# Seven-product units for retention's q/k and gates, with the residual kept in DRAM and two raw weight buffers instead of three

## The chip, the cores and the metric

One NeuronCore of a Trainium2 chip runs the whole program. The metric is device time in microseconds (us). The kernel before takes 2482.47 us (median of 3 runs, 2482.29 to 2485.35).

## What is computed

Two transformer blocks, one behind the other, on 512 tokens of width 1024, all in float32:

```python
# first block, two layers
h = h + stick_breaking_attention(rms_norm(h, g), w_sb_in, w_sb_out)
h = h + squared_relu_mlp(rms_norm(h, g), w_up, w_down)      # 1024 -> 4096 -> 1024
h = h + retention(rms_norm(h, g), w_ret_in, w_ret_out)      # 4 heads: q, k 256 wide, v and gate 512 wide
h = h + squared_relu_mlp(rms_norm(h, g), w_up, w_down)
h = rms_norm(h, g_final)
# second block
x = x + 0.5 * swiglu_ffn(x, ...)                            # hidden width 2816
x = x + mixer(x)                                            # sparse attention and mLSTM, gated
x = x + 0.5 * swiglu_ffn(x, ...)
```

## The kernel before, in words

Activations are kept transposed: tiles of 128 features by 512 tokens, in one pool of `HEAP` tiles of 2 KB a partition (L25). Every float32 operand is split into a high and a low part, and a product is three matmuls (`mm3`, L124 to L127: hi by lo, lo by hi, hi by hi).

**Weights.** `build` (L1667) lists all weight panels in the order of their use. A panel is 1 MB as a rule and is loaded by SP into one of `RAWS` raw buffers of 8 KB a partition (`load_ahead`, L193, L201). `prep` (L216) makes the high part on ACT (L240) and the low part on DVE (L241), in two halves of 1024 columns.

**A direct unit** (`g_unit`, L284) multiplies one 1024 x 128 block of weights by all 512 tokens: 8 x 3 = 24 matmuls of 512 columns. Two of them use up a panel.

**A seven-product unit** (`w_unit`, L326) does the same two blocks at once by a Strassen-Winograd scheme on 2 x 2 blocks: 7 products of 4 x 3 matmuls with 256 columns, accumulated in four PSUM banks (`w_banks`, L293, all four `z` banks). It needs sums of weight quarters and sums of activation halves. The weight sums are made partly by DMA: four loads on SP (L206 to L209), then two accumulating DMAs on POOL (L210, L211), which wait for the loads and give S1 and S3; then two DVE sums (L263) for S2 and S4. ACT (L272) and DVE (L232) split each of the seven operands. `prep` may run `WAHEAD` = 5 products ahead. The activation sums (`T`, 16 heap tiles for 1024 features) are made at the head of a stage by `w_operands` (L302): lift, four DVE sums of 256 columns, two ACT and two DVE operations of 512 (L319, L320), four times.

**Where each is used.** In each MLP (L539) the first of four groups of eight up-units is direct, and `w_operands` is spread over it, one step every `WT` = 3 atoms (an atom is three matmuls, or six in a seven-product unit); groups 1 to 3 are seven-product. In each SwiGLU (`ffn`, L995) the first `GC` = 4 gate/up pairs are direct, the other 18 are seven-product. Retention (`ret`, L853) is all direct: for each head `proj` (q, k by `g_unit`, v by `g_tokens`) and `gate` (four `g_unit`), with a `chain` woven in at one step every 4 atoms: six steps of `scores`, then sixteen of `values`, of which the last two are the row sums (L444) and, after a reciprocal square root on DVE, their spread (L437). What is left of a chain when the next head's `proj` ends is run at once (`drain`). `out(0)` (heads 0 and 1) comes after `gate(2)`, `out(1)` at the end; both add to the residual tiles `hh` (L894).

The order written in the code is a priority: the framework's scheduler issues each engine's instructions as their inputs, and the heap or raw slots they write, come free; an engine then runs them in that fixed order. A slot is taken by the first write to a tile. At the start the input `x` is loaded into two tiles of the raw pool (L1718), between the pieces of the first panel.

Of the kernel before, what the change touches and what calls it, by code (L numbers as in the profile page):

```python
# [7 lines left out]
F32 = mybir.dt.float32  # L8
# [7 lines left out]
S = 512  # L16
D = 1024
KT = 8
# [3 lines left out]
DROP = -3.3e38  # L22
FAR = -1.0e30

HEAP = 70  # L25
HALVES = 4
RAWS = 3
DEPTH = 2
LAG = 4
N1 = 6  # L30
# [24 lines left out]

WAHEAD = 5

WT = 3

GC = 4  # L60


CHUNKS = {
# [23 lines left out]
class Builder:  # L87
    def __init__(self, tc, d, out, pools):
        self.tc, self.nc, self.d, self.out = tc, tc.nc, d, out
        self.cp, self.wp, self.hp, self.sp, self.pp = pools  # L90
# [12 lines left out]
        self.uid = 0  # L103
        self.stop_at = None
# [176 lines left out]
        self.pos += 1  # L281
        return p

    def g_unit(self, name, X, w=None):  # L284
        w = w or self.next(name)
        ps = self.ps("m")
        n = len(X)
        for k in range(n):
            self.mm3(ps, w[:, k * 128:(k + 1) * 128], X[k], k == 0, k == n - 1)
            yield  # L290
        self.last = ps
# [66 lines left out]
                    yield  # L358
        self.later(done[3], c, lag=1)

    def g_tokens(self, name, X, done):

        pss = [self.ps("z" if i == ZT else "m") for i in range(4)]
# [175 lines left out]
    def mlp(self, layer, hh, X, box, nxt):  # L539

        nc = self.nc
        st = {}
        self.norm_soon(st, box)
        U = {}


        def up_done(m, ps):
            z = self.h()
            nc.scalar.activation(z, ps, AF.Relu)
            nc.scalar.activation(z, z, AF.Square)  # L550
# [36 lines left out]
        banks = self.w_banks(X[0].hi)  # L587

        def main():
            for grp in range(4):  # L590
                for m in range(0, 8, 2):
                    if grp == 0:
                        for x in range(2):
                            yield from self.g_unit(f"up{layer}", X[::2] + X[1::2])
                            self.later(up_done, m + x, self.last)
                    else:
                        yield from self.w_unit(f"up{layer}", T, banks, pair_done(m))
                if grp == 0:
                    for _ in ops:
                        pass  # L600
                self.flush()
                W = [U[m] for m in range(8)]
                for m in range(8):
                    yield from self.g_unit(f"dn{layer}", W)
                    self.later(down_done, grp, m, self.last)

        self.weave(main(), [[ops, WT]])
        self.flush()

# [240 lines left out]
                                         fill=0.0, base=0, channel_multiplier=-1)  # L850


    def ret(self, hh, X, box, nxt):  # L853
        nc = self.nc
        st = {}
        self.norm_soon(st, box)
        cs, sn = self.h(), self.h()
# [6 lines left out]
        self.later(tables, lag=N2)  # L864
        Q, V, G, SC, Y = {}, {}, {}, {}, {}

        def rotate(h, which, p1, p2):
            f = 1.0 if which == 0 else 1.0 / 16
            ts = [self.h() for _ in range(4)]
            for t, p, c in zip(ts, (p1, p2, p1, p2), (cs, sn, sn, cs)):  # L870
                nc.vector.scalar_tensor_tensor(t, p, f, c, ALU.mult, ALU.mult)
            nc.vector.tensor_tensor(ts[0], ts[0], ts[1], ALU.subtract)
            nc.vector.tensor_tensor(ts[2], ts[2], ts[3], ALU.add)
            Q[h, which] = [self.split(ts[0]), self.split(ts[2])]

        def v_done(h):
            def done(tt, ps):
# [7 lines left out]
                self.later(ev)  # L885
            return done

        def g_done(h, c, ps):
            f = G[h, c] = self.h()
            nc.vector.tensor_tensor(f, ps, st["R"], ALU.mult)  # L890
            nc.scalar.activation(f, f, AF.Silu)
# [6 lines left out]
        def scores(h):  # L898
# [20 lines left out]
        def values(h):  # L919
            sq = []  # L920
            for et in range(4):
                ps = self.ps("z")
# [25 lines left out]
        def out(pair):  # L948
            W = [Y[2 * pair + x, et] for x in range(2) for et in range(4)]
            for m in range(8):  # L950
                yield from self.g_unit("reto", W)
                self.later(out_done, pair == 1, m, self.last)

        def proj(h):
            for which in range(2):
                yield from self.g_unit("retqk", X)
                p1 = self.last
                yield from self.g_unit("retqk", X)
                self.later(rotate, h, which, p1, self.last)
            yield from self.g_tokens("retv", X, v_done(h))  # L960

        def gate(h):
            for c in range(4):
                yield from self.g_unit("retg", X)
                self.later(g_done, h, c, self.last)

        def chain(h):
            yield from scores(h)
            while (h, 3) not in G:
                yield  # L970
            yield from values(h)

# [694 lines left out]
    def build(self):  # L1667
# [8 lines left out]

        def mlp(l):
            for g in range(4):
                P(f"up{l}", range(g * 4, g * 4 + 4), g > 0)
                P(f"dn{l}", range(g * 4, g * 4 + 4))  # L1680

        def ffn(w):
# [6 lines left out]

        mlp(0)  # L1690
        for h in range(4):
            P("retqk", [2 * h, 2 * h + 1])
            P("retv", [2 * h, 2 * h + 1])
            P("retg", [2 * h, 2 * h + 1])
            if h >= 2:
                P("reto", range((h - 2) * 4, (h - 2) * 4 + 4))
        mlp(1)
# [15 lines left out]
        P("wo", range(4))  # L1713
        ffn(2)

        self.setup()

        self.xraw = [self.wp.tile([128, 2048], F32, name="raw", tag="raw", bufs=RAWS) for _ in range(2)]  # L1718
# [37 lines left out]
        if stop == "mlp0":  # L1756
            return hh
        X, Y = [], X
        self.ret(hh, Y, box, ready("mlp1", X, hh))
        if stop == "ret":  # L1760
            return hh

# [22 lines left out]

        def residual():
            R1 = self.bcast(st["r1"])
            for kt in range(KT):
                nc.vector.scalar_tensor_tensor(hh[kt], hh[kt], self.g("fin", kt), R1, ALU.mult, ALU.mult)
        self.later(two_norms, lag=N1)  # L1790
        self.later(spread_r, lag=N2)
        X, Y = [], X
# [41 lines left out]
def layout(x, w_sb_in, w_sb_out, w_ret_in, w_ret_out, g_mix, g_mlp, w_mlp_up, w_mlp_down, g_final,  # L1834
# [33 lines left out]
    d["retqk"] = full(qk.reshape(1024, 2048))  # L1868
    d["retv"] = _tok(w[:, 2048:4096])
    d["retg"] = full(w[:, 4096:])  # L1870
# [55 lines left out]
def trace(tc, d, out, stop=None, manual=False):  # L1926
    import contextlib

    with contextlib.ExitStack() as st:
        pool = lambda name, **kw: st.enter_context(tc.tile_pool(name=name, **kw))  # L1930
        pools = (pool("const", bufs=1), pool("weights", bufs=2), pool("heap", bufs=HEAP), pool("small", bufs=24),
                 pool("psum", bufs=1, space=bass.MemoryType.PSUM))
        if manual:
            st.enter_context(tc.manual_schedule())
        b = Builder(tc, d, out, pools)
# [21 lines left out]
```

## Time and profile before

| | |
|---|---|
| median of 3 runs | 2482.47 us |
| the profiled execution: time, span | 2483.38 us, 2481.7 us |
| TensorE (PE) busy | 2458.5 us, 99% of the span, 13679 matmuls |
| VectorE (DVE) busy | 1723.5 us, 69% |
| ScalarE (ACT) busy | 1253.1 us, 50% |
| GpSimd (POOL) busy | 138.1 us, 6% |
| DMA | 273.20 MB, mean 110 GB/s |

Busy times of PE are modelled (matmuls overlap one another), so its speed is read from the starts of successive matmuls. The time of an execution is 1.7 us longer than the span, which is from the first to the last instruction.

### The profile page before, as it was taken

The page shows a single profiled execution, that of the slowest core. Times are in us where ns is not written, and L with a number is a line of the kernel's source. Part 1 is how long each engine was busy: PE and PEld are TensorE (multiplying, and loading weights), DVE is VectorE, ACT ScalarE, POOL GpSimd, SP SyncE. Part 2 cuts the span into 40 slices and gives each one's busy share as a digit, 9 for nine tenths or more (in the row PEclk, how much of TensorE's full clock was granted, in tenths as well). Part 3 has the DMA queues.
Part 4 walks back from the last instruction along what each step waited for, and adds up shares of the span by engine and source line. Part 5 has one row for each costly group of instructions (what it writes and reads, how often), then busy time and mean ns, then how long its engine had stood idle before and what let it go on. Part 6 is the DMA issues. An engine that isn't in the chain of part 4 may idle for free.

```text
span 2481.7 us, 35229 instructions
## 1 busy us (share of the span) xinstructions
PE 2458.5 (99%) x13679; PEld 2141.8 (86%) x13679; DVE 1723.5 (69%) x3061; ACT 1253.1 (50%) x2160; POOL 138.1 (6%) x242
## 2 busy tenths in 40 slices
PE   9999999999999999999999999999999999999999
PEld 7888789989888888889989899998877888899998
DVE  7878857657655545657657776768799777666765
ACT  6777655436333323445436544545555454544543
POOL 0000000000000000000000001010000000001010
PEclk9999999999999999999999999999999999999999
DMA  4112144444222222244443445553221122445551
GB/s 172 69 52 85 51 136 129 127 140 131 95 89 86 76 85 98 76 132 131 129 132 127 119 139 158 148 151 115 73 85 68 51 69 85 123 141 157 150 149 73
DMA packets 78511, 273.20 MB, mean 110 GB/s; under 512 B 8836, under 2 KB 9220, under 8 KB 60680
## 3 DMA queue, kind: packets, MB, share of 16 engines
q1 hardware_dynamic: 60912, 239.43, 27.4%
q0 software_dynamic: 17280, 31.46, 7.7%
q8 instruction: 107, 1.75, 0.3%
q14 instruction: 60, 0.49, 0.1%
q10 hardware_dynamic: 152, 0.06, 0.0%
HBM read 268.82 MB, written 2.10 MB: 109 GB/s over the span
## 4 chain that ended last, share of the span: by engine, by line
PE 93%; DVE 3%; ACT 2%; issue 1%; DMA 0%; SPq 0%; DVEq 0%; ACTq 0%
PE ps_m L125 20%; PE ps_m L126 20%; PE ps_m L127 20%; PE ps_z L125 9%; PE ps_z L127 9%; PE ps_z L126 9%; PE ps_z L134 1%; PE ps_z L796 1%; PE ps_o L437 1%; DVE wlo L241 1%; PE ps_z L135 1%; PE ps_z L797 1%; PE ps_o L444 1%; ACT whi L240 0%; DVE h L1399 0%
## 5 line engine op out<-in xcount | busy, mean ns | idle before, releaser
L125 PE MATMUL ps_m<-h,whi 128*128 128x512 f32 (+1 forms) x2114 | 831.2, 393 | 7.1 <-DVE h L1191 3.5
L126 PE MATMUL ps_m<-h,wlo 128*128 128x512 f32 (+1 forms) x2114 | 826.0, 391 | 0.0
L127 PE MATMUL ps_m<-h,whi 128*128 128x512 f32 (+1 forms) x2114 | 825.0, 390 | 0.0
L240 ACT ACTIVATE whi<-raw 128x1024 fp32r<-128x1024 f32 (+2 forms) x297 | 309.7, 1043 | 580.8 <-PE ps_m L127 493.4
L125 PEld LDWEIGHTS ps_m<-h,whi 128*128 128x128 f32 x2114 | 398.1, 188 | 89.3 <-issue 6.6
L241 DVE TENSOR_TENSOR wlo<-raw,whi 128x1024 fp32r<-128x1024 f32 (+2 forms) x297 | 357.0, 1202 | 166.2 <-ACT whi L240 131.8
L127 PEld LDWEIGHTS ps_m<-h,whi 128*128 128x128 f32 x2114 | 398.1, 188 | 83.3
L126 PEld LDWEIGHTS ps_m<-h,wlo 128*128 128x128 f32 x2114 | 398.5, 189 | 76.9 <-issue 1.2
L125 PE MATMUL ps_z<-h,whi 128*128 128x256 f32 x840 | 237.8, 283 | 1.2 <-ACT h L345 1.2
L125 PE MATMUL ps_z<-h,wlo 128*128 128x256 f32 x840 | 237.7, 283 | 0.0
L126 PE MATMUL ps_z<-h,wlo 128*128 128x256 f32 x840 | 237.7, 283 | 0.0
L127 PE MATMUL ps_z<-h,whi 128*128 128x256 f32 x840 | 237.7, 283 | 0.0
L127 PE MATMUL ps_z<-h,wlo 128*128 128x256 f32 x840 | 237.7, 283 | 0.0
L126 PE MATMUL ps_z<-h,whi 128*128 128x256 f32 x840 | 237.7, 283 | 0.0
L125 PEld LDWEIGHTS ps_z<-h,whi 128*128 128x128 f32 x840 | 161.2, 192 | 1.8 <-ACT h L345 1.4
L126 PEld LDWEIGHTS ps_z<-h,whi 128*128 128x128 f32 x840 | 161.2, 192 | 0.4
L125 PEld LDWEIGHTS ps_z<-h,wlo 128*128 128x128 f32 x840 | 161.3, 192 | 0.0
L126 PEld LDWEIGHTS ps_z<-h,wlo 128*128 128x128 f32 x840 | 161.3, 192 | 0.0
L127 PEld LDWEIGHTS ps_z<-h,wlo 128*128 128x128 f32 x840 | 161.3, 192 | 0.0
L127 PEld LDWEIGHTS ps_z<-h,whi 128*128 128x128 f32 x840 | 161.2, 192 | 0.0
L580 DVE TENSOR_TENSOR h<-ps_m,h 128x512 f32<-128x512 f32 x64 | 44.3, 692 | 152.7 <-PE ps_m L127 152.7
L272 ACT ACTIVATE wlo<-raw 128x512 fp32r<-128x512 f32 x120 | 75.0, 625 | 148.8 <-PE ps_m L126 127.9
(338 smaller groups left out, 3664.8 us busy)
## 6 DMA issues: line engine op xcount, KB each, us to landing
raw<-dn SPq DMA_DIRECT2D x32, 1024.0 KB, 4.8
raw<-gu SPq DMA_DIRECT2D x72, 256.0 KB, 4.4
raw<-gu SPq DMA_DIRECT2D x36, 512.0 KB, 4.4
raw<-fd SPq DMA_DIRECT2D x16, 1024.0 KB, 4.8
raw<-up SPq DMA_DIRECT2D x48, 256.0 KB, 4.5
raw<-up SPq DMA_DIRECT2D x24, 512.0 KB, 4.5
raw<-gu POOLq DMA_DIRECT2D x36, 256.0 KB, 4.1
h<-gu SPq DMA_DIRECT2D x36, 256.0 KB, 4.7
```

Source lines behind the costliest of these rows:

```text
L125: mm(ps, lhs.hi, rhs.lo, start=first, stop=False, skip_group_check=skip)
L126: mm(ps, lhs.lo, rhs.hi, start=False, stop=False, skip_group_check=skip)
L127: mm(ps, lhs.hi, rhs.hi, start=False, stop=last, skip_group_check=skip)
L134: mm(ps, stack, rhs.lo, start=first, stop=False)
L135: mm(ps, stack, rhs.hi, start=False, stop=last)
L240: nc.scalar.activation(hi[:, a:b], r[:, a:b], AF.Copy)
L241: nc.vector.tensor_tensor(lo[:, a:b], r[:, a:b], hi[:, a:b].bitcast(F32), ALU.subtract)
L272: self.nc.scalar.activation(t[:, 0:512], src, AF.Copy)
L437: self.nc.tensor.matmul(ps[:p, tt * 128:(tt + 1) * 128], cols(tt), self.ident, start=tt == 0, stop=tt == 3)
L444: self.nc.tensor.matmul(ps[:, c:c + n], src[:, tt * 128:(tt + 1) * 128], rhs, start=first and tt == 0, stop=last and tt == 3, skip_group_c ...
L580: nc.vector.tensor_tensor(t, ps, st["R2"], ALU.mult)
L796: mm(dst, lhs, src.lo[:, s0:s1], start=False, stop=False, skip_group_check=True)
```

## The change

- Retention's q and k of heads 1 to 3 (6 pairs of units) and all its gates (8 pairs) become seven-product units. `w_operands` is woven into `proj(0)`. New evictions `qk_pair` and `g_pair` put the halves together. The `z` banks belong to these units, `g_tokens` and `out`; `scores` and `values` use the three `m` banks.
- The residual (8 tiles) is written to DRAM after `proj(0)` and read back, one or two tiles a unit, in `out(0)`.
- `RAWS` 3 to 2, `HEAP` 70 to 74.
- The direct heads are halved: 4 instead of 8 up-units in each MLP (2 more pairs seven-product), 2 instead of 4 pairs in each SwiGLU; `WT` 3 to 2.
- In the first SwiGLU the eight residual scalings are spread by due times instead of being issued together.

```diff
-HEAP = 70
+HEAP = 74
-RAWS = 3
+RAWS = 2
-WT = 3
-GC = 4
+WT = 2
+GC = 2
...
-                    if grp == 0:
+                    if grp == 0 and m < 2 * GC:
                         for x in range(2):
                             yield from self.g_unit(f"up{layer}", X[::2] + X[1::2])
                             self.later(up_done, m + x, self.last)
+                        if m == 2 * GC - 2:
+                            for _ in ops:
+                                pass
                     else:
                         yield from self.w_unit(f"up{layer}", T, banks, pair_done(m))
...
+        T = []
+        ops = self.w_operands(X, T, lift)
+        banks = self.w_banks(X[0].hi)
+        XA = X[::2] + X[1::2]
...
+        def qk_pair(h, which):
+            lo, hi = slice(0, 256), slice(256, 512)
+            p1, p2 = self.h(), self.h()
+
+            def d21(c21):
+                nc.scalar.activation(p2[:, lo], c21, AF.Copy)
+                rotate(h, which, p1, p2, -1.0)
+            return (lambda c11: nc.scalar.activation(p1[:, lo], c11, AF.Copy),
+                    lambda p, q: nc.vector.tensor_tensor(p1[:, hi], p, q, ALU.add),
+                    lambda p, q: nc.vector.tensor_tensor(p2[:, hi], p, q, ALU.add), d21)
+
+        def g_pair(h, c):
+            lo, hi = slice(0, 256), slice(256, 512)
+            R = st["R"]
+            y, z = G[h, c], G[h, c + 1] = self.h(), self.h()
+
+            def second(t, p, q, g):
+                nc.vector.tensor_tensor(t[:, hi], p, q, ALU.add)
+                nc.vector.scalar_tensor_tensor(t[:, hi], t[:, hi], g, R[:, hi], ALU.mult, ALU.mult)
+
+            def d11(c11):
+                nc.vector.tensor_tensor(y[:, lo], c11, R[:, lo], ALU.mult)
+
+            def d12(p, q):
+                second(y, p, q, 1.0)
+                nc.scalar.activation(y, y, AF.Silu)
+
+            def d21(c21):
+                nc.vector.scalar_tensor_tensor(z[:, lo], c21, -1.0, R[:, lo], ALU.mult, ALU.mult)
+                nc.scalar.activation(z, z, AF.Silu)
+                DONE.add((h, c))
+            return d11, d12, lambda p, q: second(z, p, q, -1.0), d21
...
-                z = self.ps("z")
+                z = self.ps("m")
...
+                for x in range(m, min(m + 2, 8)):
+                    if hh[x] is None:
+                        hh[x] = self.h()
+                        nc.sync.dma_start(out=hh[x], in_=self.spill[x])
+                yield from self.g_unit("reto", W, ps=banks[m % 4])
...
+                if h == 0:
+                    yield from self.g_unit("retqk", XA)
+                    p1 = self.last
+                    yield from self.g_unit("retqk", XA)
+                    self.later(rotate, h, which, p1, self.last)
+                else:
+                    yield from self.w_unit("retqk", T, banks, qk_pair(h, which))
+            yield from self.g_tokens("retv", X, v_done(h), banks)
...
-            for c in range(4):
-                yield from self.g_unit("retg", X)
-                self.later(g_done, h, c, self.last)
+            for c in (0, 2):
+                yield from self.w_unit("retg", T, banks, g_pair(h, c))
...
-        self.weave(proj(0))
+        self.weave(proj(0), [[ops, WT]])
+        for _ in ops:
+            pass
         self.flush()
+
+        for m in range(8):
+            nc.sync.dma_start(out=self.spill[m], in_=hh[m])
+        hh[:] = [None] * 8
...
+                self.later(one, kt, lag=6 * kt + 6)
```

## Rows read from the trace of the kernel before

**Rows 1.** The page: busy time by engine.

```profile
PE 2458.5 (99%) x13679; PEld 2141.8 (86%) x13679; DVE 1723.5 (69%) x3061; ACT 1253.1 (50%) x2160; POOL 138.1 (6%) x242
```

**Rows 2.** Waits of PE, longest first (us in total, times, longest us).

```profile
PE ps_o L1728 <- DMA raw<-xT: 4.1, 1, 4.1
...
PE ps_m L842 <- DVE h L807: 3.2, 2, 2.1
```

**Rows 3.** Timeline of PE, direct units (start us, us): first, last of 130.

```profile
609.68 0.39 PE L125 MATMUL ps_m<-h,whi 128*128 128x512 f32 x1
...
638.92 0.39 PE L125 MATMUL ps_m<-h,whi 128*128 128x512 f32 x1
```

**Rows 4.** Timeline of PE, an MLP's seven-product units: first, last of 83.

```profile
394.74 0.28 PE L125 MATMUL ps_z<-h,wlo 128*128 128x256 f32 x1
...
404.58 0.28 PE L126 MATMUL ps_z<-h,whi 128*128 128x256 f32 x1
```

**Rows 5.** DVE groups by shape (busy us, mean ns): splits, weight sum, 256-column eviction.

```profile
L241 DVE TENSOR_TENSOR wlo<-raw,whi 128x1024 fp32r<-128x1024 f32 x278 | 339.6, 1222 | 158.9 <-ACT whi L240 130.9 <-PE ps_z L127 26.2 <-issue 0.7
L232 DVE TENSOR_TENSOR whi<-raw,whi 128x512 fp32r<-128x512 f32 x120 | 82.3, 687 | 20.6 <-ACT whi L272 16.9
L263 DVE TENSOR_TENSOR h<-raw 128x512 f32<-128x512 f32 x60 | 41.0, 684 | 0.0
L565 DVE TENSOR_TENSOR h<-ps_z,h 128x256 f32<-128x256 f32 x24 | 10.1, 423 | 4.1 <-ACT h L345 4.1
```

**Rows 6.** Windows: A:B us, PE, PEld, DVE, ACT, POOL busy, clock, DMA share, GB/s.

```profile
709.00:788.00 79.00, 79.00 (x378) 66.65 (x377) 44.48 (x76) 28.92 (x43) 0.20 (x1) 1.00 0.24 84
2265.00:2335.00 70.00, 70.00 (x586) 70.00 (x585) 60.00 (x111) 45.68 (x90) 8.63 (x10) 1.00 0.60 168
1041.20:1064.90 23.70, 23.70 (x113) 19.70 (x112) 17.08 (x39) 16.91 (x27) 0.00 (x0) 1.00 0.25 90
1382.30:1406.00 23.70, 23.37 (x115) 19.44 (x114) 18.63 (x53) 13.29 (x20) 2.59 (x3) 1.00 0.42 122
280.00:287.00 7.00, 6.42 (x16) 5.07 (x17) 3.10 (x5) 1.50 (x4) 0.00 (x0) 0.53 0.00 0
```

**Rows 7.** Timeline of DVE, second MLP's head: `w_operands`, ends of quarters 2 and 4.

```profile
1058.36 0.69 DVE L320 TENSOR_TENSOR h<-h 128x512 fp32r<-128x512 f32 x1
...
1074.67 0.69 DVE L320 TENSOR_TENSOR h<-h 128x512 fp32r<-128x512 f32 x1
```

**Rows 8.** Timeline, the start: SP's loads, ACT's and DVE's splits, PE's second panel.

```profile
4.56 2.84 SPq L1724 DMA_DIRECT2D raw<-xT  x4
11.37 1.22 DVE L241 TENSOR_TENSOR wlo<-raw,whi 128x1024 fp32r<-128x1024 f32 x1 [0.56 <-ACT whi L240]
12.62 0.33 SPq L201 DMA_DIRECT2D raw<-sbv  x1
17.41 1.07 ACT L240 ACTIVATE whi<-raw 128x1024 fp32r<-128x1024 f32 x1 [0.50 <-DMA raw<-sbv]
20.22 0.50 PE L125 MATMUL ps_m<-wlo,h 128*128 128x512 f32 x1 [0.46 <-DVE wlo L241]
```

**Rows 9.** Timeline in the second SwiGLU: a panel's first load, S1's split, its accumulating DMA.

```profile
2290.00 0.33 SPq L206 DMA_DIRECT2D raw<-gu  x1
2292.12 0.61 ACT L272 ACTIVATE wlo<-raw 128x512 fp32r<-128x512 f32 x1
2294.13 0.86 POOL L210 DMA_DIRECT2D raw<-gu  x1 [5.81 <-DVE h L263]
```

**Rows 10.** DMA issues (count, KB each, median us to landing); last, L210's own (min, median, max).

```profile
raw<-dn SPq DMA_DIRECT2D x32, 1024.0 KB, 4.8
DMA to landing us min/median/max: 3.5/4.1/5.3
```

**Rows 11.** Timeline of PE: row sums and spread of a retention head.

```profile
997.16 0.95 PE L444 MATMUL ps_o<-ones,h 128*128 128x1 f32 x8
1000.64 1.13 PE L437 MATMUL ps_o<-ident,c 128*128 128x128 f32 x8
```

More of the change, by code (lines that the diff above doesn't have):

```diff
@@ L89, in __init__ @@
         self.tc, self.nc, self.d, self.out = tc, tc.nc, d, out
-        self.cp, self.wp, self.hp, self.sp, self.pp = pools
+        self.cp, self.wp, self.hp, self.sp, self.pp, self.dp = pools
         self.seq = []
@@ L282, in next, with g_unit @@
         return p
-    def g_unit(self, name, X, w=None):
+    def g_unit(self, name, X, w=None, ps=None):
         w = w or self.next(name)
-        ps = self.ps("m")
+        ps = self.ps("m") if ps is None else ps
         n = len(X)
@@ L359, in w_unit, with g_tokens @@
         self.later(done[3], c, lag=1)
-    def g_tokens(self, name, X, done):
-        pss = [self.ps("z" if i == ZT else "m") for i in range(4)]
+    def g_tokens(self, name, X, done, pss=None):
+        pss = pss or [self.ps("z" if i == ZT else "m") for i in range(4)]
         for s in range(4):
@@ L595, in main @@
                             self.later(up_done, m + x, self.last)
+                        if m == 2 * GC - 2:
+                            for _ in ops:
+                                pass
                     else:
                         yield from self.w_unit(f"up{layer}", T, banks, pair_done(m))
-                if grp == 0:
-                    for _ in ops:
-                        pass
                 self.flush()
@@ L850, in keep, with ret @@
                                          fill=0.0, base=0, channel_multiplier=-1)
-    def ret(self, hh, X, box, nxt):
+    def ret(self, hh, X, box, nxt, lift):
         nc = self.nc
+        T = []
+        ops = self.w_operands(X, T, lift)
+        banks = self.w_banks(X[0].hi)
+        XA = X[::2] + X[1::2]
         st = {}
@@ L865, in ret, with rotate @@
         Q, V, G, SC, Y = {}, {}, {}, {}, {}
-        def rotate(h, which, p1, p2):
+        def rotate(h, which, p1, p2, sign=1.0):
             f = 1.0 if which == 0 else 1.0 / 16
             ts = [self.h() for _ in range(4)]
-            for t, p, c in zip(ts, (p1, p2, p1, p2), (cs, sn, sn, cs)):
-                nc.vector.scalar_tensor_tensor(t, p, f, c, ALU.mult, ALU.mult)
+            for t, p, c, g in zip(ts, (p1, p2, p1, p2), (cs, sn, sn, cs), (f, f * sign, f, f * sign)):
+                nc.vector.scalar_tensor_tensor(t, p, g, c, ALU.mult, ALU.mult)
             nc.vector.tensor_tensor(ts[0], ts[0], ts[1], ALU.subtract)
@@ L874, in rotate @@
             Q[h, which] = [self.split(ts[0]), self.split(ts[2])]
+        def qk_pair(h, which):
[24 more added lines that the diff above has]
+            return d11, d12, lambda p, q: second(z, p, q, -1.0), d21
+        DONE = set()
         def v_done(h):
@@ L921, in values @@
             for et in range(4):
-                ps = self.ps("z")
+                ps = self.ps("m")
                 for ch in "ABC":
@@ L950, in out @@
             for m in range(8):
-                yield from self.g_unit("reto", W)
+                for x in range(m, min(m + 2, 8)):
[3 more added lines that the diff above has]
+                yield from self.g_unit("reto", W, ps=banks[m % 4])
                 self.later(out_done, pair == 1, m, self.last)
@@ L955, in proj @@
             for which in range(2):
[L956 to L960, printed above, removed]
+                if h == 0:
[6 more added lines that the diff above has]
+            yield from self.g_tokens("retv", X, v_done(h), banks)
         def gate(h):
-            for c in range(4):
-                yield from self.g_unit("retg", X)
-                self.later(g_done, h, c, self.last)
+            for c in (0, 2):
+                yield from self.w_unit("retg", T, banks, g_pair(h, c))
         def chain(h):
             yield from scores(h)
-            while (h, 3) not in G:
+            while (h, 2) not in DONE:
                 yield
@@ L1678, in mlp @@
             for g in range(4):
-                P(f"up{l}", range(g * 4, g * 4 + 4), g > 0)
+                for i in range(g * 4, g * 4 + 4):
+                    P(f"up{l}", [i], i >= GC)
                 P(f"dn{l}", range(g * 4, g * 4 + 4))
@@ L1691, in build @@
         for h in range(4):
-            P("retqk", [2 * h, 2 * h + 1])
+            P("retqk", [2 * h, 2 * h + 1], h > 0)
             P("retv", [2 * h, 2 * h + 1])
-            P("retg", [2 * h, 2 * h + 1])
+            P("retg", [2 * h, 2 * h + 1], True)
             if h >= 2:
@@ L1714, in build @@
         ffn(2)
+        self.spill = [self.dp.tile([128, S], F32, name="spill", tag="spill") for _ in range(KT)]
         self.setup()
@@ L1758, in build @@
         X, Y = [], X
-        self.ret(hh, Y, box, ready("mlp1", X, hh))
+        self.ret(hh, Y, box, ready("mlp1", X, hh), lambda k: self.lifted(hh[k], self.g("mix1", k)))
         if stop == "ret":
@@ L1787, in residual, with one @@
             R1 = self.bcast(st["r1"])
+            def one(kt):
+                nc.vector.scalar_tensor_tensor(hh[kt], hh[kt], self.g("fin", kt), R1, ALU.mult, ALU.mult)
             for kt in range(KT):
-                nc.vector.scalar_tensor_tensor(hh[kt], hh[kt], self.g("fin", kt), R1, ALU.mult, ALU.mult)
+                self.later(one, kt, lag=6 * kt + 6)
         self.later(two_norms, lag=N1)
@@ L1867, in layout @@
     qk = np.concatenate([w[:, :1024].reshape(1024, 4, 256), w[:, 1024:2048].reshape(1024, 4, 256)], axis=2)
-    d["retqk"] = full(qk.reshape(1024, 2048))
+    d["retqk"] = full(apart(qk.reshape(1024, 2048)))
     d["retv"] = _tok(w[:, 2048:4096])
-    d["retg"] = full(w[:, 4096:])
+    d["retg"] = full(apart(w[:, 4096:]))
     d["reto"] = full(w_ret_out[0])
@@ L1931, in trace @@
         pools = (pool("const", bufs=1), pool("weights", bufs=2), pool("heap", bufs=HEAP), pool("small", bufs=24),
-                 pool("psum", bufs=1, space=bass.MemoryType.PSUM))
+                 pool("psum", bufs=1, space=bass.MemoryType.PSUM), pool("dram", bufs=KT, space=bass.MemoryType.DRAM))
         if manual:
```

4 lines of the change are left out of this document (removed).

## The prediction

> **What bounds the kernel now.** Read the page first: PE is busy for 99% of the span, DVE for 69% [rows 1]. PE's busy time is modelled and may hide gaps, so the waits of PE come next: the longest in the whole program is 4.1 us, the very first load of x, and the next are smaller [rows 2]. PE is never short of weights or operands for long: 2481.7 - 2458.5 = 23 us of idling in all. So the speed of its stream is the bound, and that is read from starts in the timeline. In direct units 129 steps take 638.92 - 609.68 = 29.24 us, 0.2267 us a matmul of 512 columns [rows 3]. In seven-product units 82 steps take 404.58 - 394.74 = 9.84 us, 0.1200 us a matmul of 256 [rows 4]. The third view is the windows: where seven-product units run back to back, DVE is busy 60.00 of 70 us; over one retention head, 44.48 of 79 [rows 6]. There is room on DVE in retention, little elsewhere.
>
> **What it removes.** A pair of blocks costs 2 x 24 x 0.2267 = 10.88 us directly and 84 x 0.1200 = 10.08 us by seven products, so 0.80 us less, not an eighth: the narrow matmul carries as large a fixed part as the wide one. Pairs changed: 6 of q/k, 8 of gates, 2 x 2 in the MLPs, 2 x 2 in the SwiGLUs, 22 in all. 22 x 0.80 = 17.6 us. Two dummy matmuls of `w_banks` give 2 x 0.2267 = 0.5 back. **17.1 us** is what PE's stream loses.
>
> A rule speaks for more. The Trainium skill, TensorE: Matmul & The Clock Gate, section "Wait — 56ns, not 53.3ns?", has successive warm matmuls N ÷ 2.4 GHz + about 2.5 ns apart. By that rule, an estimate, 215.8 and 109.2 ns, 1.19 us a pair and 26 us for the 22. The trace does not agree (226.7 and 120.0 ns); the measurement decides, and the rule gets 0.01, inside the low rival below.
>
> **What it adds, and what covers it.** Everything else is off PE, so it costs only where PE runs dry.
>
> *DVE and ACT in retention.* A panel of a seven-product unit costs DVE 7 x 0.687 + 2 x 0.684 = 6.2 us where two halves of 1.22 us made 2.4 [rows 5]; four panels a head: +15. Two additions of 256 columns for each q/k pair and six operations of 256 instead of two of 512 for each gate pair: 4 x 0.42 + 2 x (6 x 0.42 - 2 x 0.69) = +4. DVE goes from 44.5 to some 64 us in a head that then takes 79 - 4 x 0.8 = 75.8: 84%, just under the 86% at which the SwiGLUs lose nothing [rows 6]. ACT, at 28.9, has more room. Cover: the five products of lead. The rotation (eight operations, 5.5 us in one piece) is the longest burst and stays under 5 x 12 x 0.12 = 7.2 us of lead. I take 1 us; bounds 0 and, if each of the six bursts overruns by 1, 6.
>
> *The chain's end.* A head's gate and the next `proj` have 28 + 60 atoms instead of 32 + 64, so 22 turns instead of 24 for 22 steps of the chain and one turn spent waiting: the spread falls into `drain`, straight behind the row sums. They are 3.5 us apart because DVE's square root lies between [rows 11]; these are the rows of head 3, which is drained already, and PE idled 0.3 us there, since the scheduler put matmuls of `out` into the gap. Bounds 0 and 3 x 3.5 = 10.5; with those rows nearest, 1 us.
>
> *The heads.* All of `w_operands` must now be issued within 4 direct units, 21.8 us plus 1.9 for norm matmuls, 23.7, instead of 34.4. In that stretch DVE was busy 17.1 us (second MLP) and 18.6 (first SwiGLU) [rows 6]. Half of `w_operands` was then still to come (quarter 4 ended at 1074.67, quarter 2 at 1058.36 [rows 7]); of that some 1.7 quarters of 4 x 0.42 + 2 x 0.69 = 3.1 us lay behind the window: +5.2. Five products' operands in lead, with two sums: +4.8. Two and a half direct splits fewer: -3.0. That is 24.1 and 25.6 us of DVE for 23.7 of PE, with 1.4 us of grace, since the first product takes `X` alone. Operations issued back to back start 0.1 us closer than they last, which eases it. Overrun between 0 and 2 us for each of four heads; I take 3 together (0 to 8). The first SwiGLU's residual scalings (eight, 5.5 us) are spread over its first units, where they burst before: nothing gained or lost.
>
> *The start, with two raw buffers.* x held two, the first panel the third. Now x's first half and the first panel (which is written to before x's second half) hold both, so x's last four tiles wait until the panel has been split: 11.37 + 1.22 = 12.6, where before they were issued from 4.56 [rows 8]. The second panel, issued at 12.62 before, goes behind four SP issues and 1 MB, and behind the squares of x's first half: some 14.5. Before, it was split from 17.41 and PE waited 0.46 us for it. Two to three us later it makes PE wait about 2.5, +2. If PE's clock falls for that, it costs 3.3 us more: behind the two waits of L842, 3.2 us together [rows 2], the granted clock was 0.53 from 280 to 287 us [rows 6], so mostly the lower level, 1.2 of 2.4 GHz, and 7 us did 3.7 us' work. Bounds 0.5 and 6; I take 3, since it is the only place where a load is plainly on the path.
>
> *The lead of the loads.* A panel's loads are issued when a buffer comes free, as before, but for the next panel rather than the one after. In the SwiGLU: freed and issued at 2290.00, POOL's accumulating DMA at 2294.13, landing 4.1 us later (3.5 to 5.3) [rows 9, 10], so S1 is there at +8.2 to +9.4. ACT took S1 of the panel then current at 2292.12, so with two buffers it wants the new one a unit later, 2292.12 + 10.08 - 2290.00 = 12.2. Slack 2.8 to 4.0 us: 0. A plain panel lands in 4.8 of the 10.9 us its predecessor lasts [rows 10]: 0. Queued behind these on SP are the 8 spills and 8 reloads (x's four took 2.84 us to issue [rows 8], so 5.7 for a row of eight; 2 MB each way) and the decay table; on POOL one memset a head. Spills collide with a load whose slack is 3 to 4 us; reloads are issued one unit (5.4 us) or more ahead and should take no more than the 4.8 us of a whole panel [rows 10]; only DVE's additions wait for them, but behind those stand the splits, with a lead of two half panels. I take 1 us (0 to 6). The heap: T takes 16 tiles, the residual gives back 8, and `HEAP` 4; what is short must be waited for, in the same 0 to 6, because PE has other products to turn to.
>
> **The sum.** 17.1 - 1 - 1 - 3 - 3 - 1 = 8.1 us less. Against the profiled execution, 2483.38 - 8.1 = 2475.3; the median of the runs lies 0.9 below that execution, so **2474** for the median. About 0.2%, 5 us, is what a measurement of this kernel can tell from no change: faster is below 2477.5, slower above 2487.5.
>
> **The rivals.**
>
> *Nothing is exposed.* The scheduler fills every gap as it does before, and all costs but the start's 1 us vanish: 2482.5 - 16 = 2466. For it: PE's waits are nearly nil even where DVE is at 86%. Against: the start and the heads are new squeezes. 0.20.
>
> *The squeezes take it all.* DVE overruns in all four heads by 3 (12), the start costs 5 with the clock: 17.1 - 17 = 0, 2482. For it: the 24.1 and 25.6 us above against 23.7. The same size comes if the chain's end is not filled (10.5). 0.23.
>
> *Two buffers are one too few.* S1 comes later than the 12.2 us, ACT stands on it, and the copies between PSUM banks queued behind on ACT stop PE. It decides from the point where S1's way takes over 12.2 rather than 8.2 us. It then repeats for every seven-product panel that follows another: 20 in the MLPs, 34 in the SwiGLUs, 9 in retention, 63 in all. At 0.3 us each 19 us: 2474 + 19 = 2493, slower. Below 0.13 us each it only eats the gain. For it: the DMA share is 0.60 in such stretches [rows 6] and the longest landing 5.3. Against: even 5.3 leaves slack. 0.15.
>
> *It does not do what it says*: retention's units do not reach 0.12 us, with other matmuls between them; then a third of the gain goes, 2480. 0.02.
>
> **How the numbers follow.** The forecast, costs of 5 to 13 us and 2470 to 2477.5, has 0.40. Faster: 0.40 + 0.20 = 0.60, and 0.03 from the upper rivals where they end early: 0.63. Same 0.23, slower 0.14. The range leaves out 1 in 10 above and less below: from 2465 (all but a us or two hidden) to 2490 (the buffer rival at 0.25 us a panel).
>
> **What would show it.** 14473 matmuls; seven-product units at 0.120 us in retention; DVE near 60 to 64 us a head there. A wait of some 2 to 3 us on PE near 20 us, for the second panel. PE's waits for `w_operands` or a split at the ends of the four heads, below 2 us each. No wait of ACT's splits on DMA. It is wrong if ACT's splits in the SwiGLUs wait on accumulating DMAs, if waits of PE in retention sum to over 6 us, or if the heads cost more than their 6.4 us.

## The result: 0.95% slower, and the profile after

The changed kernel takes 2506.24 us (median of 4 runs, 2506.02 to 2508.59), the kernel before 2482.78 (4 runs, 2482.29 to 2485.35): a ratio of 1.0095 (95% interval 1.0083 to 1.0107), 23.5 us slower. The forecast was 2474, with 2490 as the upper end. The profiled execution took 2506.02 us, its span is 2504.3 us, 22.6 more than before's.

The page of the changed kernel, busy time by engine, beside [rows 1]:

```profile
PE 2452.4 (98%) x14473; PEld 2171.7 (87%) x14473; DVE 1818.2 (73%) x3311; ACT 1331.0 (53%) x2386; POOL 175.8 (7%) x286
```

The 14473 matmuls are those forecast. PE is busy 6.1 us less, and the span is longer by 22.6: PE stands idle for 29 us more. Its waits, longest first, beside [rows 2], say where:

```profile
PE ps_z L125 <- DVE h L319: 10.2, 3, 4.9
PE ps_o L444 <- DVE h L456: 6.0, 1, 6.0
...
PE ps_z L125 <- ACT ps_z L341: 4.1, 5, 2.0
...
PE ps_m L125 <- DVE h L173: 3.2, 2, 1.7
...
PE ps_o L437 <- DVE c L431: 3.1, 2, 2.5
```

New are L319 (activation sums of `w_operands`), L456 and L431 (the first norm), L173 in retention, and the copies between banks at L341. To price them by stage, both timelines are cut at the same instructions: the last L797 of the first attention and the row sums (L444) ahead of the norms of retention, the second MLP and the two SwiGLUs. First before, then after (x5 and x7 are the same eight matmuls, merged in two pieces):

```profile
275.92 0.39 PE L797 MATMUL ps_z<-h,ntri 128*128 128x512 f32 x1
...
639.61 0.61 PE L444 MATMUL ps_o<-ones,h 128*128 128x1 f32 x5
...
1045.30 0.95 PE L444 MATMUL ps_o<-ones,h 128*128 128x1 f32 x8
...
1386.39 0.95 PE L444 MATMUL ps_o<-ones,h 128*128 128x1 f32 x8
...
2134.21 0.95 PE L444 MATMUL ps_o<-ones,h 128*128 128x1 f32 x8
```

```profile
286.12 0.39 PE L797 MATMUL ps_z<-h,ntri 128*128 128x512 f32 x1
...
659.32 0.83 PE L444 MATMUL ps_o<-ones,h 128*128 128x1 f32 x7
...
1057.20 0.95 PE L444 MATMUL ps_o<-ones,h 128*128 128x1 f32 x8
...
1406.10 0.95 PE L444 MATMUL ps_o<-ones,h 128*128 128x1 f32 x8
...
2154.44 0.94 PE L444 MATMUL ps_o<-ones,h 128*128 128x1 f32 x8
```

The start (to the end of the first attention) is 286.12 - 275.92 = 10.2 us longer; the first MLP, from the first to the second cut, (659.32 - 286.12) - (639.61 - 275.92) = 9.5; retention 7.8 *shorter*, the second MLP 7.8 longer, the first SwiGLU with the mixer 0.5, the second SwiGLU 2.4: 22.6 together. So retention did gain; the start and the two MLPs, where the change only clears room for it or goes along with it, lost more.

**The start.** Timeline of the changed kernel, beside [rows 8]:

```profile
12.65 1.75 SPq L1772 DMA_DIRECT2D raw<-xT  x4
...
15.14 1.36 ACT L490 ACTIVATE h<-raw,gains 128x512 fp32r<-128x512 f32 x2 [3.78 <-DMA raw<-xT]
...
18.83 1.66 ACT L450 ACTIVATE h<-raw 128x512 f32<-128x512 f32 x3
...
21.03 0.33 SPq L201 DMA_DIRECT2D raw<-sbv  x1
...
25.61 1.84 PE L444 MATMUL ps_o<-ones,h 128*128 128x1 f32 x8 [6.00 <-DVE h L456]
...
29.97 2.05 PE L437 MATMUL ps_o<-ident,c 128*128 128x128 f32 x8 [2.52 <-DVE c L431]
...
31.67 0.77 PE L125 MATMUL ps_m<-wlo,h 128*128 128x512 f32 x1
```

x's last four tiles wait for the first panel's split, as forecast (12.65). But the second panel's load goes out at 21.03, not 14.5: it needs the buffer of x's first half, whose squares (L450, 18.83) stand on ACT behind the gains of the last four tiles, and ACT idles 3.78 us for those. PE has used up its first panel at 19.6 and starts the second at 31.67; between them lie only the norm's matmuls. (The very first wait for x, 4.1 us before, was 5.3 in this execution; it was 4.0 in the run with a step every atom below, whose start is as late, so it is not the cause.) The windows (columns as in [rows 6]) add the granted clock: PE has 6.00 us without a matmul, up to 25.61, and from within them on the clock is at its lower level, 0.77 and then 0.50:

```profile
20.00:25.00 5.00, 0.00 (x0) 0.00 (x0) 4.38 (x7) 3.08 (x6) 0.41 (x2) 0.77 0.60 200
25.00:30.00 5.00, 1.87 (x9) 1.84 (x9) 2.63 (x15) 2.00 (x2) 0.41 (x2) 0.50 0.55 221
319.00:329.00 10.00, 10.00 (x55) 8.55 (x54) 3.42 (x7) 6.99 (x13) 0.86 (x1) 1.00 0.28 50
341.00:350.00 9.00, 8.26 (x48) 7.96 (x49) 7.35 (x14) 7.29 (x17) 0.00 (x0) 0.67 0.37 120
1065.50:1087.40 21.90, 17.09 (x95) 14.64 (x93) 13.86 (x28) 15.66 (x29) 0.00 (x0) 1.00 0.08 14
```

**The MLP heads.** The last three of these windows belong to the heads: 10 us ahead of the first MLP's stall, the stretch right behind that stall, and the second MLP's head. In the first, DVE is busy 3.42 of 10 us (from there to the end of the stall, 319 to 341 us, 13.00 of 22), in the second MLP's head 13.86 of 21.9: no engine is full, yet PE waits for DVE. The timeline of the second head shows why:

```profile
1054.95 1.32 ACT L496 ACTIVATE h<-h,gains 128x512 f32<-128x512 f32 x2
...
1065.01 0.60 ACT L473 ACTIVATE h<-ps_o 128x512 f32<-128x512 f32 x1 [3.36 <-PE ps_o L437]
...
1065.51 1.32 ACT L496 ACTIVATE h<-h,gains 128x512 f32<-128x512 f32 x2
...
1066.73 0.58 ACT L549 ACTIVATE h<-ps_m 128x512 f32<-128x512 f32 x1
...
1069.05 0.69 DVE L173 TENSOR_TENSOR h<-h 128x512 fp32r<-128x512 f32 x1 [0.49 <-ACT h L172]
...
1069.66 0.42 DVE L310 TENSOR_TENSOR h<-h 128x256 f32<-128x256 f32 x1
...
1071.24 0.63 ACT L316 ACTIVATE h<-h 128x512 fp32r<-128x512 f32 x1 [2.22 <-DVE h L312]
...
1072.30 1.32 ACT L496 ACTIVATE h<-h,gains 128x512 f32<-128x512 f32 x2
...
1075.46 0.69 DVE L173 TENSOR_TENSOR h<-h 128x512 fp32r<-128x512 f32 x1 [2.26 <-ACT h L172]
...
1080.61 1.32 ACT L496 ACTIVATE h<-h,gains 128x512 f32<-128x512 f32 x2
...
1083.77 0.69 DVE L173 TENSOR_TENSOR h<-h 128x512 fp32r<-128x512 f32 x1 [2.06 <-ACT h L172]
...
1086.62 0.69 DVE L319 TENSOR_TENSOR h<-h 128x512 fp32r<-128x512 f32 x1
...
1087.37 0.39 PE L125 MATMUL ps_z<-h,wlo 128*128 128x256 f32 x1 [4.02 <-DVE h L319]
```

A quarter of `w_operands` is a relay: lifts on ACT (L496), four sums on DVE (from L310), two copies on ACT (L316), two subtractions on DVE (L319). From one quarter's lifts to the next pass 10.6, 6.8 and 8.3 us, while a direct unit takes 5.4, and the last quarter is 4.02 us late. In the first of these gaps ACT stands 3.36 us at the copy of the norm's spread (L473), which waits for PE. In the others an eviction of a direct unit stands between lifts and sums on both queues (L549 on ACT, L173 on DVE), a relay itself: DVE waits 2.26 and 2.06 us at L173 for ACT.

The Trainium skill (Perfetto Trace Analysis, "Identifying the Most-Contended Engine") takes the occupancy of VectorE and ScalarE as a fair measure of how close they are to roofline. By that measure neither is close to it in the second head (13.86 and 15.66 of 21.9 us), and PE waits all the same: here occupancy does not tell whether a chain across both is in time.

### The profile page after: what moved, and what is told of

Its sections match the earlier page's. It is cut to its first block, busy times and chain, and to the rows that moved or that the text cites. A ratio compares the mean times of both kernels' runs of the same rounds, so it can differ in the third digit from the quotient of the medians.

```text
span 2504.3 us, 37668 instructions
## 1 busy us (share of the span) xinstructions
PE 2452.4 (98%) x14473; PEld 2171.7 (87%) x14473; DVE 1818.2 (73%) x3311; ACT 1331.0 (53%) x2386; POOL 175.8 (7%) x286
## 4 chain that ended last, share of the span: by engine, by line
PE 88%; DVE 6%; ACT 3%; DMA 1%; issue 1%; SPq 0%; DVEq 0%; ACTq 0%; POOLq 0%
PE ps_m L125 15%; PE ps_m L126 14%; PE ps_m L127 14%; PE ps_z L125 13%; PE ps_z L127 13%; PE ps_z L126 13%; PE ps_z L796 1%; DVE wlo L241 1%; PE ps_z L797 1%; PE ps_z L134 1%; PE ps_o L444 1%; PE ps_z L135 1%; PE ps_o L437 1%; DMA raw<-gu 1%; DVE h L173 0%
## 5 line engine op out<-in xcount | busy, mean ns | idle before, releaser
L125 PE MATMUL ps_m<-h,whi 128*128 128x512 f32 x1634 | 642.9, 394 | 6.5 <-DVE h L1237 3.5
L126 PE MATMUL ps_m<-h,wlo 128*128 128x512 f32 x1634 | 638.1, 391 | 0.0
L127 PE MATMUL ps_m<-h,whi 128*128 128x512 f32 x1634 | 637.8, 390 | 0.0
L125 PE MATMUL ps_z<-h,whi 128*128 128x256 f32 (+1 forms) x1276 | 378.4, 297 | 7.5 <-ACT ps_z L341 4.1
L127 PE MATMUL ps_z<-h,whi 128*128 128x256 f32 (+1 forms) x1276 | 375.9, 295 | 0.0
L126 PE MATMUL ps_z<-h,wlo 128*128 128x256 f32 (+1 forms) x1276 | 375.6, 294 | 0.0
L125 PEld LDWEIGHTS ps_m<-h,whi 128*128 128x128 f32 x1634 | 307.7, 188 | 71.4 <-issue 6.6
L127 PEld LDWEIGHTS ps_m<-h,whi 128*128 128x128 f32 x1634 | 307.5, 188 | 64.2
L126 PEld LDWEIGHTS ps_m<-h,wlo 128*128 128x128 f32 x1634 | 307.9, 188 | 59.8 <-issue 2.1
L125 PE MATMUL ps_z<-h,wlo 128*128 128x256 f32 x1148 | 326.8, 285 | 10.2 <-DVE h L319 10.2
L126 PE MATMUL ps_z<-h,whi 128*128 128x256 f32 x1148 | 326.2, 284 | 0.6 <-DVE whi L232 0.6
L127 PE MATMUL ps_z<-h,wlo 128*128 128x256 f32 x1148 | 325.6, 284 | 0.0
L125 PEld LDWEIGHTS ps_z<-h,whi 128*128 128x128 f32 x1276 | 245.2, 192 | 16.6 <-ACT ps_z L341 5.3
L127 PEld LDWEIGHTS ps_z<-h,whi 128*128 128x128 f32 x1276 | 245.4, 192 | 5.1
L126 PEld LDWEIGHTS ps_z<-h,wlo 128*128 128x128 f32 x1276 | 245.2, 192 | 4.7
L125 PEld LDWEIGHTS ps_z<-h,wlo 128*128 128x128 f32 x1148 | 221.1, 193 | 11.7 <-DVE h L319 11.3
L126 PEld LDWEIGHTS ps_z<-h,whi 128*128 128x128 f32 x1148 | 221.4, 193 | 1.7 <-DVE whi L232 0.8
L127 PEld LDWEIGHTS ps_z<-h,wlo 128*128 128x128 f32 x1148 | 221.0, 193 | 0.0
```

Of the source, the lines that this page charges most:

```text
L125: mm(ps, lhs.hi, rhs.lo, start=first, stop=False, skip_group_check=skip)
L126: mm(ps, lhs.lo, rhs.hi, start=False, stop=False, skip_group_check=skip)
L127: mm(ps, lhs.hi, rhs.hi, start=False, stop=last, skip_group_check=skip)
```

## The experiments

All times are medians; the ratio is to the kernel before on the same chip. That kernel took 2482.14 to 2482.78 us beside the other runs and 2483.88 beside the last three, so between those three and the rest a difference of 1.5 us in the medians means nothing; the ratios allow for it. The stages are cut as above; each entry is us more than the kernel before in the profiled execution. A row sum can be placed some matmuls earlier or later, so an entry is good to about 2 us.

| kernel | median | ratio (95%) | start | MLP 1 | retention | MLP 2 | SwiGLU 1, mixer | SwiGLU 2 |
|---|---|---|---|---|---|---|---|---|
| changed | 2506.24 | 1.0095 (1.0083 to 1.0107) | 10.2 | 9.5 | -7.8 | 7.8 | 0.5 | 2.4 |
| squares first | 2501.42 | 1.0078 (1.0063 to 1.0093) | 5.5 | 9.7 | -7.6 | 7.7 | 0.1 | 5.6 |
| x in heap | 2501.97 | 1.0078 (1.0063 to 1.0093) | 5.9 | 10.3 | -7.9 | 8.1 | 0.4 | 1.2 |
| long heads | 2484.35 | 1.0007 (0.9998 to 1.0017) | 11.6 | 0.5 | -7.0 | 0.2 | -1.1 | -0.6 |
| before, short heads | 2509.34 | 1.0108 (1.0093 to 1.0123) | 0.1 | 10.6 | 0.0 | 7.8 | 7.2 | 0.3 |
| before, two buffers | 2495.28 | 1.0050 (1.0036 to 1.0064) | 10.5 | -1.8 | 0.0 | 0.0 | 0.5 | 0.3 |
| a step every atom | 2492.71 | 1.0041 (1.0027 to 1.0055) | 10.9 | 6.6 | -7.0 | 0.2 | -0.4 | -1.4 |
| start and long heads | 2473.51 | 0.9966 (0.9954 to 0.9978) | -0.1 | -0.6 | -7.3 | 0.0 | -1.7 | -0.6 |
| middle heads | 2472.99 | 0.9960 (0.9946 to 0.9974) | 0.8 | 0.7 | -7.6 | -0.7 | -1.9 | -1.7 |
| scaling spread | 2468.69 | 0.9944 (0.9931 to 0.9956) | -0.6 | -1.2 | -11.5 | 0.0 | -2.3 | -0.7 |
| chain every three | 2471.03 | 0.9950 (0.9937 to 0.9964) | -0.3 | -0.8 | -10.6 | 0.0 | -2.1 | -0.4 |
| residual in one piece | 2474.89 | 0.9966 (0.9953 to 0.9978) | -0.2 | -0.6 | -7.0 | 0.0 | 2.3 | -0.7 |

### Squares first

```diff
-        for kt in range(KT):
-            t = self.xraw[kt // 4][:, (kt % 4) * 512:(kt % 4 + 1) * 512]
-            X.append(self.gain_in(t, self.g("mix0", kt)))
...
-        for kt in range(KT):
-            self.sumsq(box, kt, self.xraw[kt // 4][:, kt % 4 * 512:kt % 4 * 512 + 512])
+        for half in range(2):
+            for kt in range(4 * half, 4 * half + 4):
+                t = self.xraw[kt // 4][:, (kt % 4) * 512:(kt % 4 + 1) * 512]
+                X.append(self.gain_in(t, self.g("mix0", kt)))
...
+            for kt in range(4 * half, 4 * half + 4):
+                self.sumsq(box, kt, self.xraw[kt // 4][:, kt % 4 * 512:kt % 4 * 512 + 512])
...
```

> The changed kernel, but at the start the squares of x's first four tiles are written ahead of the products with the gains of its last four. Theory (order on ACT): in the changed kernel the second panel's load is issued at 21.03 us, when the squares of the first four tiles have let go of their raw buffer; these squares stand on ACT behind gains that wait 3.8 us for x's last tiles. With the squares ahead the load should go out near 14 to 15 us and PE should wait 2 to 4 us for that panel instead of the 6.00 + 2.52 us and the row of slow matmuls behind them: 6 to 8 us less, 2498 to 2500. Rival (the second panel is late because x's last tiles, 1 MB, come late, whatever the order): the wait stays, 2505 to 2507.

Measured: 4.8 us less, half of the start's loss, so less than expected. The load now goes out at 15.02, as expected, and PE's wait for the norm falls from 6.00 to 3.39. But the panel's split stands on ACT behind the other four squares and begins only at 22.07. So the order on ACT is a cause, and this order mends half of the loss.

### x's second half in the heap

```diff
-        self.xraw = [self.wp.tile([128, 2048], F32, name="raw", tag="raw", bufs=RAWS) for _ in range(2)]
+        raw = self.wp.tile([128, 2048], F32, name="raw", tag="raw", bufs=RAWS)
+        self.xraw = [raw[:, kt * 512:kt * 512 + 512] for kt in range(4)] + [self.h() for _ in range(4)]
```

> The changed kernel, but x's last four tiles are loaded into the heap, so the start needs only one raw buffer beside the first panel's. Theory: the start goes back to that of the kernel before (second panel issued near 12.6 us), and everything to the end of the first attention moves by the 10.2 us by which it is late now: 9 to 10 us less, 2496 to 2497. Rival (two buffers cost at every panel, the start is only the first place where it shows): the start gains 3 to 5, and the rest of the 10 us stays.

Measured: 4.3 us less, a miss. The second panel's load does go out at 12.83, but with four heap tiles created ahead of the products, the scheduler put the first product with a gain behind three weight splits on ACT, at 11.45 instead of 4.09 in the kernel before. This run exchanged one wait for another and decides nothing on the cause; the wait it bought, in PE's timeline:

```profile
12.21 0.79 PE L125 MATMUL ps_m<-wlo,h 128*128 128x512 f32 x1 [5.16 <-ACT h L490]
```

### Long heads

```diff
-WT = 2
-GC = 2
+WT = 3
+GC = 4
```

> The changed kernel with the long heads of the kernel before (four pairs direct in each SwiGLU, eight direct units in each MLP, one step of the activation sums every three atoms). Theory (the sums of one quarter are a chain ACT, DVE, ACT, DVE of some 6.8 us, behind an eviction on both queues, while a direct unit lasts 5.4): the long head hides it, and the stages get back what they lost against the kernel before, 11.3 + 7.8 us in the two MLPs and 0.9 + 2.4 in the SwiGLUs: 22 us less, 2484. Rival (two raw buffers bring the first seven-product panels late): the waits at the heads stay, less than 6 us is won, above 2500.

Measured: 21.9 us less, as the chain has it. All waits for L319 are gone, and both MLPs and both SwiGLUs are within 1.1 us of before. (The 11.3 us that the expectation has for the first MLP are counted from a later cut, the row sums ahead of that MLP's norm, where the changed kernel is 8.45 us late; the table counts from the end of the attention, where it is 10.2 late, and has 9.5.)

### The kernel before with short heads

```diff
-WT = 3
-GC = 4
+WT = 2
+GC = 2
```

(with the loops of the change in the MLP and its order of panels, and the residual's scalings left in one piece)

> The kernel before, with three raw buffers and direct retention, with only the short heads (two pairs direct in each SwiGLU, four direct units in each MLP, a step of the activation sums every two atoms). Theory of the chain: the short heads alone cost what they cost in the changed kernel, 19 us in the MLPs and 3 in the SwiGLUs: 2503 to 2505. Rival (two raw buffers are what makes the heads late): with three buffers the short heads save their 6.4 us or lose a little of it, 2476 to 2482. Rival (DVE's sum of work in the head, 24.1 and 25.6 us for 23.7): about even, 2482 to 2486.

Measured: 27.2 us more than before, more than expected. The short heads alone cost the MLPs 10.6 and 7.8, with three buffers and direct retention. The 7.2 in the first SwiGLU, where the changed kernel has 0.5, goes by the trace with the residual: its eight scalings in one piece hold DVE for 5.38 us from 1434.98, ACT stands 4.91 us behind them and then PE 5.3. No run changes the residual alone under short heads, so this size is read from the trace and not tested.

```profile
PE ps_z L125 <- DVE h L319: 10.4, 3, 4.7
PE ps_z L125 <- ACT h L345: 5.3, 1, 5.3
```

### The kernel before with two buffers

```diff
-HEAP = 70
-RAWS = 3
+HEAP = 74
+RAWS = 2
```

> The kernel before with two raw buffers instead of three and 74 heap tiles instead of 70, and nothing else. Theory: two buffers cost at the start alone, some 10 us there, and nothing at the seven-product panels: 2491 to 2494, with all stages behind the first attention as long as before. Rival of the prediction (S1 comes late in every seven-product panel): the MLPs and SwiGLUs grow too, 2497 and more. Rival (free): 2482.

Measured: 12.9 us more, and 9.4 in the profiled execution, the fastest of the four. There all of it is at the start: SP's load at 21.03 and PE's wait of 6.07 us for L456 are there again, and every stage with seven-product panels is within 0.5 us of before, or shorter. Where the slower executions lose 2 to 4 us more no trace shows. The prediction's slower rival, S1 late in each panel, is out.

### A step of the activation sums every atom

```diff
-WT = 2
+WT = 1
```

> The changed kernel with its short heads, but one step of the activation sums after every atom instead of every second one, so that the quarters are written ahead of the evictions of the direct units. Theory (a quarter waits on ACT's and DVE's queues behind evictions that wait for PE; DVE stood idle 6.5 us of the 10 before the stall): the same sum of work, in another order, takes most of the 19 us of the two MLPs back: 8 to 15 us less, 2491 to 2498. Rival (DVE has too much work for the 23.7 us of the head): the order changes nothing, 2504 to 2508.

Measured: 13.5 us less, with the same instructions in another order. No wait of PE for L319 is left. The second MLP loses nothing any more: with the sums ahead of the evictions, its lifts follow one another after 5.3, 4.4 and 5.5 us.

```profile
1053.59 1.32 ACT L496 ACTIVATE h<-h,gains 128x512 f32<-128x512 f32 x2
...
1058.91 1.32 ACT L496 ACTIVATE h<-h,gains 128x512 f32<-128x512 f32 x2
...
1063.28 1.32 ACT L496 ACTIVATE h<-h,gains 128x512 f32<-128x512 f32 x2
...
1068.76 1.32 ACT L496 ACTIVATE h<-h,gains 128x512 f32<-128x512 f32 x2
```

The first MLP still loses 6.6, with a wait of 2.96 us for a weight split on ACT (to 335.98); there, too, DVE is not full, busy 10.34 of the 17.38 us ahead of it. So it is order, not the sum of DVE's work. But the short heads save nothing this way either.

### The start mended, and long heads

```diff
-WT = 2
-GC = 2
+WT = 3
+GC = 4
...
+            elif kt == 4:
+                for j in range(4, KT):
+                    xs.append(self.h())
+                    nc.sync.dma_start(out=xs[j], in_=self.d["xT"][j])
...
```

> The changed kernel with the long heads, and with x's last four tiles loaded into heap tiles that are taken behind the first four products with the gains. Theory: two separate losses, the start (11.6 us behind the kernel before at the end of the first attention when only the heads are long again) and the heads; with both gone, what retention saves is left: 2484.35 - 10 to 11.6, 2473 to 2475, faster than the kernel before by 7 to 9 us. Rival (two raw buffers cost the start anyhow, since the panels behind the first one come late too): 2479 to 2482.

Measured: 2473.51, 8.8 us faster than before: what remains is retention's 7.3, 1.7 in the first SwiGLU with the mixer, and some tenths elsewhere. With the heap tiles taken behind the first four products, ACT keeps its order and the start is that of before, with two buffers.

The edits of the four runs below are shown against this one.

### Heads of middle length

```diff
-GC = 4
+GC = 3
```

> As the run with the long heads and the mended start, but heads of middle length: three pairs direct in each SwiGLU, six direct units in each MLP, one step every three atoms. Theory (four quarters of 6.8 to 8 us behind a norm of 10 need about six units of 5.4 us, 32.6): nearly hidden, the four pairs save up to 3.2 us: 2470 to 2475. If the chain is longer than that, PE waits 1 to 4 us in each head and its clock falls: 2476 to 2485.

Measured: 2472.99, not to be told from the long heads. PE waits for the sums (L319) just once, 0.6 us, but the 3.2 us saved do not show either; with two or three us of scatter in the start and the first MLP this stays open.

### Retention: the scaling spread

```diff
             for et in range(4):
-                nc.vector.tensor_tensor(G[h, et], G[h, et], rs, ALU.mult)
-                Y[h, et] = self.split(G[h, et])
+                if h < 2:
+                    self.later(scale, et, lag=6 * et + 6)
+                else:
+                    scale(et)
```

(`scale` holds the two lines taken out)

> The changed kernel with long heads and the mended start (2473.5), and in retention the scaling of heads 0 and 1 by their norm (four products and four splits on DVE, 5.5 us in one piece behind the chain that is drained) spread over the next units, one every six atoms. Theory: this burst stands ahead of the next head's first scores on DVE and makes PE wait 1.5 and 1.7 us there (1.6 and 1.9 against its pace): 2 to 3.5 us less, 2470 to 2471.5, and both waits gone. Rival (the drain of the chain itself, not the burst): the waits stay, 2473 to 2474.

Measured: 2468.69, 4.8 us less than without it, a bit more than expected, and the fastest version here: 0.9944 (0.9931 to 0.9956) of the kernel before. Retention gains 4.2. In the changed kernel the burst of the drained head and the wait behind it, in the timeline, are these:

```profile
782.07 1.88 DVE L978 TENSOR_TENSOR h<-h,ps_o 128x512 f32<-128x512 f32 x3
...
786.26 1.29 DVE L173 TENSOR_TENSOR h<-h 128x512 fp32r<-128x512 f32 x2
...
789.46 0.68 DVE L949 TENSOR_TENSOR h<-ps_m,h 128x512 f32<-128x512 f32 x1
...
792.00 0.50 PE L125 MATMUL ps_m<-h 128*128 128x512 f32 x1 [1.48 <-DVE h L173]
```

L978 and its splits take DVE's queue from 782.07 to 787.5, the next head's scores (L949) come behind them, and PE waits 1.48 us for the scores' split. With the scaling spread, no wait for L173 is left in PE's list.

### Retention: a step of the chain every three atoms

```diff
-c = [chain(h), 4]
+c = [chain(h), 3]
```

> As the run with long heads and the mended start, but retention's chain takes a step every three atoms instead of every four, so that it ends before the next head's projections do and nothing is left to drain. Theory of the burst: the burst comes earlier, beside direct units of v, and the waits of 1.6 and 1.9 us go: 2 to 3.5 us less, 2470 to 2471.5. If scores and values then want DVE in the seven-product units of the same head, new waits take it back: 2473 to 2476.

Measured: 2471.03, 2.5 us less, retention 3.3 shorter, with one wait of 0.6 us for L173 left. Both ways of getting the burst out of the scores' way work. The spread may be the better one (the intervals overlap).

### The residual in one piece

```diff
-                self.later(one, kt, lag=6 * kt + 6)
+                one(kt)
```

> As the run with long heads and the mended start, but the eight scalings of the residual in the first SwiGLU come in one piece again, as in the kernel before. Theory: with the long head they cost what the kernel before shows there, one wait of 1.21 us and some slow clock, 1 to 3.5 us more: 2474.5 to 2477, lost in the first SwiGLU. By the prediction (nothing gained or lost): 2473 to 2474.

Measured: 2474.89, 1.4 us more, which the medians cannot tell from nothing: the ratio is 0.9966 in both. The trace does have a difference: waits for L345, one of them 1.2 us as before the change, are back, and the first SwiGLU with the mixer is 4.0 us longer than with the spread. But the profiled execution was the slowest of its five, so what the spread is worth with long heads stays open.

## Why the prediction was wrong

**The stream: right.** Seven-product units keep 0.120 us a matmul in retention. 14 pairs by 0.80, less the dummies, are 10.7 us; retention gains 11.5 once nothing stands in its way. DVE was forecast at 60 to 64 us a head; one head's window has a little less, and the stretch from row sums to row sums (774.66 to 851.95 us) has 59.99:

```profile
703.40:780.70 77.30, 77.30 (x531) 72.41 (x530) 57.62 (x112) 44.93 (x87) 7.37 (x10) 1.00 0.50 138
```

**The start: forecast 3 us (0.5 to 6), was 10.2.** The failed step is "behind the squares of x's first half: some 14.5". The squares were counted as if they ran when their data was there. They stand behind the gains of the second half in ACT's fixed order, and those wait for the very transfer that was being delayed. So the load came at 21.03.

**The heads: forecast 3 us for all four (0 to 8), were some 27.** This is the largest step that failed: "24.1 and 25.6 us of DVE for 23.7 of PE". With 3 here, the sum below would be 0.4: no change instead of slower. Work was added up for one engine and held against PE's time. What counts is the relay of ACT and DVE, behind the norm's copy that waits for PE and behind evictions that are relays themselves. Of the prediction's own signs of being wrong, "if the heads cost more than their 6.4 us" is the one that came. Between the changed kernel and long heads the stages differ by 9.0, 7.6, 1.6 and 3.0 us, and the 6.4 us that the short heads should save are lost on top: 27.6 (no run shows the 6.4 by itself). The change of order alone (a step every atom) took half of it back. [Rows 7] were read as a pace that `WT` could set at will: two quarters in 16.3 us, 8.2 each, are just 12 atoms of 0.68. How close quarters *can* follow one another these rows do not show, and no bound was put on it; they were then asked to follow at 5.4. (The trace of before has lifts 9.4, 5.6 and 10.3 us apart in that head; the short head made it 10.6, 6.8 and 8.3, and only another order 4.4 to 5.5.)

**The chain's end: forecast 1 us (0 to 10.5), were 3.5.** The place was right, the mechanism not: not the 3.5 us between row sums and spread, but the scaling behind the spread, which keeps DVE from the next head's scores (1.6 and 1.9 us against PE's pace in heads 1 and 2).

**DVE's load in retention and the loads' lead: forecast 1 us each; nothing found.** With the scaling spread, retention has its whole gain, spills and reloads included; the two buffers cost nothing at the panels.

**The residual: "nothing gained or lost".** With short heads the trace puts some 6.7 us on it (7.2 in one piece, 0.5 spread, in kernels that differ in more than that); with long heads the gain is not shown clear of noise.

The sum with these sizes: 17.1 - 10.2 - 27.6 - 3.5 = -24.2, against -22.6 in the profiled executions. The rival that held 0.23, "the squeezes take it all", named both places and put 12 and 5 us on them. The slower rival gave S1's lateness as its reason, which did not happen; it is no credit to it that the kernel came out slower.

## What to carry to other kernels

Where work is to be hidden behind a stretch of another engine, add up not only each engine's busy time but the longest chain across engines, and write down what stands ahead of each link on its queue. A queue that runs in a fixed order makes an early-ready instruction as late as the latest one in front of it, so an edit that delays one transfer delays all that is queued behind its consumer. And try the parts of a large change one by one: the part that was made for the gain gained; two that looked like small change cost three times as much.

## What the runs showed that was not expected

PE loses time behind a wait as well as in it: after the first MLP's head had stalled for 4.9 us, the granted clock was 0.67 from 341 to 350 us, so at the lower of its two levels for two thirds of them; in the start, where 6.00 us without a matmul end at 25.61, it was 0.50 from 25 to 30 us, the lower level throughout. And two raw buffers, with loads that land in 3.9 to 5.6 us (medians of the DMA issues), were enough for every panel behind the start: with them alone, in the kernel before, no later stage is more than 0.5 us longer.
